# Last down projection: sixteen 128x512 additions and multiplications from VectorE to GpSimd, and a normalisation cut in two

## The chip, the cores and the metric

The program runs on one core of a Trainium2 chip. The metric is the device time of one execution in microseconds, as the median of several runs. Five engines work side by side, each through its own queue in order: TensorE (PE) multiplies matrices, VectorE (DVE) and GpSimd (POOL) work element by element, ScalarE (ACT) applies functions with a scale and a bias, and SyncE (SP) issues transfers. They wait for one another by semaphores.

## The reference, cut to what matters

The reference is a trunk of two layers on 1024 rows of 1024 features. Each layer mixes the rows (a gated delta net, then retention), normalises, runs a feed-forward block with a convolution, and normalises again:

```
gate, up = jnp.split(h @ w_up, 2, axis=-1)
gate = causal_dwconv(gate, conv_w) + conv_b
y = (jax.nn.silu(gate) * up) @ w_down
x = layer_norm(DN_ALPHA * x + (1.0 + g2) * y, ln_g[i, 1], ln_b[i, 1])
```

The change is in the last two lines of the last layer: the product with `w_down` (2816 x 1024), the residual sum, and the layer norm whose result is the output.

## The kernel before, in words

The down projection is `proj_gen`. It makes the product by seven block products in the manner of Strassen (`prods`), on halves of the rows (half 0: rows 0 to 511, half 1: rows 512 to 1023), of the contraction and of the columns (nh 0: columns 0 to 511, nh 1: 512 to 1023). Each product runs over 11 steps j. A step loads a block of activations (`ar`) and makes a block of weights (`Br`, differences of loaded blocks, L1521), and splits each into a high and a low part: ScalarE rounds (L89) to the high part, VectorE subtracts (L90) to get the low part. These pairs are `ab` and `bb`. Four row tiles t of 128 rows then take three matmuls each (L1636), so a step has 12 matmuls. In the last product the first five steps run step by step over all tiles; the last six are kept back and run tile by tile, 18 matmuls to a tile, so that tile 0 is finished first.

What becomes of the products, with the names that matter here:

- The fifth product ends half 0: `f3` and `finish(0, t, 1, ...)` add the residual and make statistics (L1565), then `norm(0, t)` normalises tile t of half 0 and stores it.
- The sixth product (`f7`) gives the right columns of half 1: ScalarE copies the accumulator to `u2` (L1617), VectorE adds it to `p5` (L1618, the tile is called `pa`), and `finish(1, t, 1, p5)` multiplies by the gain row (L1562), adds the residual (L1564) and makes statistics (L1565).
- The seventh product (`f4`) gives the left columns of half 1 in the accumulators `acc`, which lie in PSUM. `finish(1, t, 0, acc)` and `norm(1, t)` follow tile by tile. These are the last steps of the program.

`norm` in the last layer, for one tile: join the statistics (L1570), add epsilon (L1571), GpSimd raises the variance to the power -1/2 (L1572, one element to a partition), VectorE makes a bias (L1578). The left half of the columns (`lo`) is done by VectorE in two passes (L1581, L1582) and stored (L1583). The right half (`hi`) is normalised by ScalarE (L1580), then VectorE multiplies by the gain row (L1584) and adds the bias row (L1585), and it is stored (L1586). The tiles `xt`, `pa`, `rowb`, `ab`, `bb`, `u2` and `mv` lie in SBUF; `acc`, `sc` and `mm` in PSUM.

The order on each engine is not the order of the code. A scheduler sets it when the program is built: it takes instructions out of order where it expects their inputs earlier, and the engines then follow that order whatever really comes first.

Of the kernel before, what the change touches and what calls it, by code (L numbers as in the profile page):

```python
# [12 lines left out]
ALU = mybir.AluOpType  # L13
# [20 lines left out]
def trunk_kernel(ctx: ExitStack, tc, A):  # L34
    nc = tc.nc
    pe, act, dve, pool, sp = nc.tensor, nc.scalar, nc.vector, nc.gpsimd, nc.sync
# [9 lines left out]
    def tl(tag, shape, dt=F32, name=None):  # L46
        return sb.tile(shape, dt, tag=tag, name=name or tag, bufs=BUFS[tag])
# [34 lines left out]
    def hs(half):  # L82
        return slice(half * HALF, (half + 1) * HALF)
# [234 lines left out]
    def normalize(xt, mv, on_act):  # L318
        if on_act:
            dve.scalar_tensor_tensor(mv[:, 2:3], mv[:, 0:1], -1.0, mv[:, 3:4], ALU.mult, ALU.mult)  # L320
            act.activation(xt, xt, AF.Identity, bias=mv[:, 2:3], scale=mv[:, 3:4])
        else:
            dve.tensor_scalar(xt, xt, mv[:, 0:1], mv[:, 3:4], ALU.subtract, ALU.mult)
# [335 lines left out]
    xt = [[tl("lane", [P, 2, HALF], name="xt") for _ in range(4)], [[None, None] for _ in range(4)]]  # L659
# [817 lines left out]
    def proj_gen(nj, ablk, wsrc, slots, xsrc, G, final, ln_next, tag, ltags, dst, key, mm=pe.matmul, gate=None):  # L1477
# [3 lines left out]
        p5 = [pa[2 + t // 2][:, t % 2] for t in range(4)]  # L1481
        u2 = []
# [57 lines left out]
        xts = [[], []]  # L1540
# [16 lines left out]
        def xh(half, t, nh):  # L1557
            x = xts[half][t]
            return x[nh] if isinstance(x, tuple) else x[:, hs(nh)]

        def finish(half, t, nh, c):
            dve.tensor_tensor(c, c, G[nh], ALU.mult)  # L1562
            xv = xh(half, t, nh)
            dve.scalar_tensor_tensor(xv, xv, ALPHA, c, ALU.mult, ALU.add)  # L1564
            dve.bn_stats(stats[half][t][:, nh], xv)  # L1565

        def norm(half, t):
            xt = xts[half][t]
            mv = tl("s8", [P, 4], name="mv")
            dve.bn_aggr(mv[:, 0:2], stats[half][t])  # L1570
            dve.tensor_scalar(mv[:, 2:3], mv[:, 1:2], LN_EPS, None, ALU.add)  # L1571
            pool.tensor_tensor(mv[:, 3:4], mv[:, 2:3], mhalf[:, 0:1], ALU.pow)  # L1572
            if final is None:
                normalize(xt, mv, bal["n"] & 1 << half)
            else:
                (gB, bB), out = final
                r0 = half * HALF + t * P
                dve.scalar_tensor_tensor(mv[:, 2:3], mv[:, 0:1], -1.0, mv[:, 3:4], ALU.mult, ALU.mult)  # L1578
                lo, hi = xh(half, t, 0), xh(half, t, 1)
                act.activation(hi, hi, AF.Identity, bias=mv[:, 2:3], scale=mv[:, 3:4])  # L1580
                dve.scalar_tensor_tensor(lo, lo, mv[:, 0:1], gB[0], ALU.subtract, ALU.mult)  # L1581
                dve.scalar_tensor_tensor(lo, lo, mv[:, 3:4], bB[0], ALU.mult, ALU.add)  # L1582
                sp.dma_start(out[r0:r0 + P, hs(0)], lo)  # L1583
                dve.tensor_mul(hi, hi, gB[1])  # L1584
                dve.tensor_add(hi, hi, bB[1])  # L1585
                sp.dma_start(out[r0:r0 + P, hs(1)], hi)  # L1586

        c11, later = [], []

# [21 lines left out]
        def f3(t, acc):  # L1611
            dve.tensor_add(u2[t], acc, u2[t])
            later.append(lambda: finish(0, t, 1, u2[t]))
            later.append(lambda: norm(0, t))

        def f7(t, acc):
            act.activation(u2[t], acc, AF.Copy)  # L1617
            later.append(lambda: dve.tensor_add(p5[t], u2[t], p5[t]))  # L1618
            if gate:
                later.append(lambda: dve.tensor_add(p5[t], p5[t], p1[t]))  # L1620
            later.append(lambda: finish(1, t, 1, p5[t]))

        def f4(t, acc):
            if gate:
                dve.tensor_add(acc, acc, p1[t])
            finish(1, t, 0, acc)
            norm(1, t)

        outs = []
        prods = [("11", "11", f1, 0, True), ("12", "21", f2, 1, True), ("S1", "T1", f5, 1, True),  # L1630
                 ("S2", "T2", f6, 0, bool(gate)), ("S4", "22", f3, 1, False), ("S3", "T3", f7, 0, False),
                 ("22", "T4", f4, 0, False)]
        banks = [None, None]

# [95 lines left out]
    def layer_tail(i, mix, wout, xsrc, x_mid, x_out, ln_next, final):  # L1730
# [101 lines left out]
        if not final:  # L1832
            wnext_up.append(A["ret_wg"][2])
        gb2 = gain_rows(3, ("mid", i), "hTb") if final else None
        return proj_st(proj_gen(NF // 2, ablk_of(ad, "qkv"), A["ffn_down"][i], slots, xg[i + 1], rows[i, 5],
                       (gb2, x_out) if final else None, ln_next, "hTb", ("hTb", "hTa", 8, 6, "f") if final else ("qkv", "hTa", 8, 4, "0"), x_out, ("out", i)))

# [19 lines left out]
    h0, xts = layer_tail(0, raws, A["gdn_wout"], xin, xs[0], xs[1], next0, False)  # L1857
# [230 lines left out]
    def start_out():  # L2088
        slots = {"c": "hTb", "x": "hTb"}
        mix.append(proj_gen(8, ablk_of(od, "qkv"), A["ret_wout"], slots, xg[0], rows[1, 2], None,  # L2090
                            lambda: mix[1], "hTa", ("qkv", "hTb", 4, 4, "r"), xs[2], ("mid", 1), pm, lambda j: after_ev(("ob", j // 2))))
        assert next(mix[0]) == "ops"
# [131 lines left out]
```

## Time and profile before

| | us |
|---|---|
| median of 3 runs | 2862.41 |
| lowest and highest of them | 2862.29, 2869.69 |
| the profiled execution's own time | 2866.75 |
| its span, first to last instruction | 2865.0 |
| PE busy in the span | 2781.6 (97%) |
| DVE busy | 2186.8 (76%) |
| ACT busy | 1292.3 (45%) |
| POOL busy | 495.2 (17%) |

The profiled execution took 4.34 us more than the median of the runs, and 1.75 us of it lie outside its span. Busy times are averages over the program. Where a tile is named, buffer numbers are left out, so `xt` stands for all the row tiles. A timeline row reads: start, duration, engine, line, operation, output and inputs, shape, and in brackets the idle time before it and what ended it. Rows of one kind that follow each other are merged, with their count behind an x. Instructions on VectorE overlap by about 0.1 us, so the step from one start to the next is the time that one takes in a full queue.

### The profile page before, as it was taken

The page shows a single profiled execution, that of the slowest core. Times are in us where ns is not written, and L with a number is a line of the kernel's source. Part 1 is how long each engine was busy: PE and PEld are TensorE (multiplying, and loading weights), DVE is VectorE, ACT ScalarE, POOL GpSimd, SP SyncE. Part 2 cuts the span into 40 slices and gives each one's busy share as a digit, 9 for nine tenths or more (in the row PEclk, how much of TensorE's full clock was granted, in tenths as well). Part 3 has the DMA queues.
Part 4 walks back from the last instruction along what each step waited for, and adds up shares of the span by engine and source line. Part 5 has one row for each costly group of instructions (what it writes and reads, how often), then busy time and mean ns, then how long its engine had stood idle before and what let it go on. Part 6 is the DMA issues. An engine that isn't in the chain of part 4 may idle for free.

```text
span 2865.0 us, 38941 instructions
## 1 busy us (share of the span) xinstructions
PE 2781.6 (97%) x13594; PEld 2272.3 (79%) x13594; DVE 2186.8 (76%) x3874; ACT 1292.3 (45%) x2377; POOL 495.2 (17%) x517
## 2 busy tenths in 40 slices
PE   8999999999999999999999999999999999999997
PEld 6788888877787878887888887777787788888886
DVE  6797778676788888778677656666788887777869
ACT  3753465344644444545433342222344644445443
POOL 0411311000023222000000002333301033322001
PEclk9999999999999999999999999999999999999999
DMA  8223243273255554945343364665854253435843
GB/s 280 97 97 113 93 133 104 71 247 138 100 181 173 194 181 168 338 134 172 129 147 131 115 199 153 200 208 152 276 192 147 74 195 133 147 136 171 314 147 118
DMA packets 254292, 465.31 MB, mean 162 GB/s; under 512 B 24400, under 2 KB 81104, under 8 KB 254096
## 3 DMA queue, kind: packets, MB, share of 16 engines
q1 hardware_dynamic: 219776, 407.50, 43.2%
q10 hardware_dynamic: 31488, 46.15, 4.4%
q0 software_dynamic: 2832, 9.18, 0.8%
q8 instruction: 107, 1.75, 0.3%
q14 instruction: 89, 0.73, 0.1%
HBM read 346.86 MB, written 115.87 MB: 162 GB/s over the span
## 4 chain that ended last, share of the span: by engine, by line
PE 56%; DVE 22%; DMA 10%; ACT 5%; issue 4%; POOL 1%; SPq 0%; ACTq 0%; DVEq 0%; POOLq 0%
PE acc L747 7%; PE acc L1340 6%; PE acc L110 4%; PE acc L111 4%; PE acc L112 4%; PE acc L1636 4%; PE sc L747 3%; PE sc L1340 3%; DMA mvw<-in_ada_w 2%; DVE qkv L507 2%; DVE o L1787 2%; PE mm L747 2%; DVE wb L90 2%; DMA wr<-in_ffn_up 2%; DVE mm L1394 2%
## 5 line engine op out<-in xcount | busy, mean ns | idle before, releaser
L747 PE MATMUL acc<-hT,wh 128*128 128x512 f32 x960 | 298.4, 392 | 0.0
L1636 PE MATMUL acc<-bb,ab 128*128 128x512 f32 x984 | 231.3, 394 | 4.8 <-DVE ab L90 3.0
L89 ACT ACTIVATE ab<-ar 128x512 fp32r<-128x512 f32 x210 | 131.0, 630 | 222.2 <-PE mm L316 55.1
L1636 PEld LDWEIGHTS acc<-bb,ab 128*128 128x128 f32 x984 | 184.3, 189 | 46.9 <-DVE ab L90 3.1
L747 PEld LDWEIGHTS acc<-hT,wh 128*128 128x128 f32 x960 | 181.4, 189 | 35.1
L90 DVE TENSOR_TENSOR ab<-ar,ab 128x512 fp32r<-128x512 f32 x210 | 149.2, 719 | 70.4 <-ACT ab L89 67.1
L1340 PE MATMUL acc<-T,wb 128*128 128x512 f32 x840 | 202.0, 389 | 0.4 <-DVE wb L90 0.4
L89 ACT ACTIVATE wb<-mm 128x512 fp32r<-128x512 f32 x216 | 124.3, 597 | 169.6 <-DVE mm L1394 158.5
L747 PE MATMUL acc<-hT,wl 128*128 128x512 f32 x480 | 196.6, 410 | 3.6 <-DVE wl L90 2.3
L1340 PEld LDWEIGHTS acc<-T,wb 128*128 128x128 f32 x840 | 157.5, 188 | 33.8 <-ACT o L1788 1.2
L90 DVE TENSOR_TENSOR wl<-wr,wh 128x1024 fp32r<-128x1024 f32 x95 | 119.1, 1254 | 75.6 <-ACT wh L89 75.3
L89 ACT ACTIVATE wh<-wr 128x1024 fp32r<-128x1024 f32 x95 | 100.4, 1057 | 144.7 <-PE acc L747 61.3
L90 DVE TENSOR_TENSOR wb<-wr,wb 128x512 fp32r<-128x512 f32 x162 | 115.9, 716 | 64.7 <-ACT wb L89 64.5
L1818 POOL TENSOR_TENSOR o<-o 128x512 f32<-128x512 f32 x80 | 112.6, 1416 | 268.1 <-ACT pc L1410 173.9
L1787 DVE SCALAR_TENSOR_TENSOR o<-g,vc,o 128x512 f32<-128x512 f32 (+2 forms) x176 | 150.9, 868 | 7.0 <-ACT o L1782 5.8
L90 DVE TENSOR_TENSOR wb<-mm,wb 128x512 fp32r<-128x512 f32 x216 | 145.4, 686 | 7.4 <-ACT wb L89 7.4
L89 ACT ACTIVATE wb<-wr 128x512 fp32r<-128x512 f32 x162 | 101.1, 626 | 93.5 <-PE acc L1340 26.4
L1394 DVE TENSOR_TENSOR mm<-wr 128x512 f32<-128x512 f32 x108 | 86.5, 800 | 70.6 <-DMA wr<-in_ffn_up 56.8
L747 PE MATMUL acc<-wh,hT 128*128 128x512 f32 x384 | 134.8, 413 | 2.0 <-DVE vv L90 2.0
L1410 ACT ACTIVATE pc<-acc 128x512 f32<-128x512 f32 x143 | 84.3, 590 | 107.6 <-PE acc L1340 62.4
L252 DVE SCALAR_TENSOR_TENSOR ada<-mvw,e,ada 128x512 f32<-128x512 f32 x140 | 106.6, 761 | 25.2 <-DMA mvw<-in_ada_w 25.0
L110 PE MATMUL acc<-T,wb 128*128 128x512 f32 x292 | 114.4, 392 | 3.6 <-DVE wb L90 3.5
(677 smaller groups left out, 7361.5 us busy)
## 6 DMA issues: line engine op xcount, KB each, us to landing
wr<-in_ffn_up SPq DMA_DIRECT2D x92, 512.0 KB, 3.9
mvw<-in_ada_w SPq DMA_DIRECT2D x80, 512.0 KB, 4.4
ad<-o SPq DMA_DIRECT2D x154, 256.0 KB, 2.3
ar<-ad SPq DMA_DIRECT2D x154, 256.0 KB, 4.7
Br<-in_ffn_down SPq DMA_DIRECT2D x88, 256.0 KB, 5.1
wr<-in_ret_wv SPq DMA_DIRECT2D x32, 512.0 KB, 3.6
ar<-od SPq DMA_DIRECT2D x56, 256.0 KB, 4.7
wr<-in_gdn_wqkv SPq DMA_DIRECT2D x24, 512.0 KB, 3.8
```

Source lines behind the costliest of these rows:

```text
L89: anchor["sp"] = act.activation(dst_h, src, AF.Copy)
L90: eng.tensor_tensor(dst_l, src, dst_h, ALU.subtract)
L110: mm(acc, wl[:, k], hl[0], start=first, stop=False)
L111: mm(acc, wh[:, k], hl[1], start=False, stop=False)
L112: mm(acc, wh[:, k], hl[0], start=False, stop=last)
L252: dve.scalar_tensor_tensor(a, wr[:, kk], e[:, k:k + 1], a, ALU.mult, ALU.add)
L747: pq(pe.matmul(out, lhsT, rhs, start=start, stop=stop), cost or COST[out.shape[-1]])
L1340: return pe.matmul(*a, skip_group_check=True, **kw)
L1394: dve.tensor_tensor(t, x, y, op)
L1636: return pe.matmul(*args, skip_group_check=True, **kw)
L1787: dve.scalar_tensor_tensor(tv, gv[:, c0 - j:c1 - j], w[:, 2 - j:3 - j], tv, ALU.mult, ALU.add)
L1818: (dve if fp == 0 else pool).tensor_tensor(o[d], o[x], o[y], op)
```

## The change

`norm` is cut into `stat` (statistics and the power) and `apply` (the rest). Where it is the last layer, `f4` puts `apply` of a tile behind `stat` of the next tile in the code. In `apply`, the multiplication and addition on the right half go to GpSimd for the four tiles of half 0 and for tiles 0 and 1 of half 1, and stay on VectorE for tiles 2 and 3 of half 1. The addition of `u2` to `p5` in `f7` also goes to GpSimd in the last layer. That is 12 + 4 instructions of 128x512 elements.

```
-        def norm(half, t):
-            xt = xts[half][t]
+        def stat(half, t):
             mv = tl("s8", [P, 4], name="mv")
             dve.bn_aggr(mv[:, 0:2], stats[half][t])
             dve.tensor_scalar(mv[:, 2:3], mv[:, 1:2], LN_EPS, None, ALU.add)
             pool.tensor_tensor(mv[:, 3:4], mv[:, 2:3], mhalf[:, 0:1], ALU.pow)
+            return mv
+
+        def apply(half, t, mv):
+            xt = xts[half][t]
...
+                eng = dve if half and t > 1 else pool
...
-                dve.tensor_mul(hi, hi, gB[1])
-                dve.tensor_add(hi, hi, bB[1])
+                eng.tensor_tensor(hi, hi, gB[1], ALU.mult)
+                eng.tensor_tensor(hi, hi, bB[1], ALU.add)
                 sp.dma_start(out[r0:r0 + P, hs(1)], hi)
+
+        def norm(half, t):
+            apply(half, t, stat(half, t))
...
-            later.append(lambda: dve.tensor_add(p5[t], u2[t], p5[t]))
+            later.append(lambda: (pool if final else dve).tensor_tensor(p5[t], u2[t], p5[t], ALU.add))
...
             finish(1, t, 0, acc)
-            norm(1, t)
-
+            if not final:
+                norm(1, t)
+                return
+            last.append((t, stat(1, t)))
+            if t:
+                apply(1, *last.pop(0))
+            if t == 3:
+                apply(1, *last.pop(0))
+
+        last = []
```

Line numbers shift: L1571 becomes L1570, the power L1572 becomes L1571, L1578 becomes L1582, L1580 becomes L1584, L1581 and L1582 become L1585 and L1586, L1584 and L1585 become L1588 and L1589, L1618 becomes L1625.

The end of GpSimd's queue before, with the numbers of the buffers (`o` is the feed-forward block's activation, long done by then; mv_24592 to mv_24660 belong to tiles 0 to 3 of half 0, and the four that follow, from mv_25095 on, to half 1):

```order
L1818 TENSOR_TENSOR o_23120<-o_23120,o_23105 128x512
L1818 TENSOR_TENSOR o_23115<-o_23115,o_23105 128x512
L1572 TENSOR_TENSOR mv_24592<-mv_24592,mhalf_80 128x1
L1572 TENSOR_TENSOR mv_24607<-mv_24607,mhalf_80 128x1
L1572 TENSOR_TENSOR mv_24645<-mv_24645,mhalf_80 128x1
L1572 TENSOR_TENSOR mv_24660<-mv_24660,mhalf_80 128x1
L1572 TENSOR_TENSOR mv_25095<-mv_25095,mhalf_80 128x1
```

The same place in GpSimd's queue now, up to the power of the fourth tile of half 0 (xt_23795 and xt_23844 are tiles 0 and 1 of half 0, pa_23281 and pa_23282 hold `p5` of two tiles each):

```order
L1571 TENSOR_TENSOR mv_24592<-mv_24592,mhalf_80 128x1
L1571 TENSOR_TENSOR mv_24607<-mv_24607,mhalf_80 128x1
L1588 TENSOR_TENSOR xt_23795<-xt_23795,rowb_23273 128x512
L1625 TENSOR_TENSOR pa_23281<-u2_24318,pa_23281 128x512
L1625 TENSOR_TENSOR pa_23281<-u2_24326,pa_23281 128x512
L1589 TENSOR_TENSOR xt_23795<-xt_23795,rowb_23276 128x512
L1588 TENSOR_TENSOR xt_23844<-xt_23844,rowb_23273 128x512
L1625 TENSOR_TENSOR pa_23282<-u2_24334,pa_23282 128x512
L1571 TENSOR_TENSOR mv_24645<-mv_24645,mhalf_80 128x1
L1625 TENSOR_TENSOR pa_23282<-u2_24342,pa_23282 128x512
L1589 TENSOR_TENSOR xt_23844<-xt_23844,rowb_23276 128x512
L1571 TENSOR_TENSOR mv_24660<-mv_24660,mhalf_80 128x1
```

The power of tile 2 now stands behind six 128x512 instructions, that of tile 3 behind eight. Behind these rows follow the four of tiles 2 and 3 of half 0, and then, between the powers of half 1, the four of its tiles 0 and 1.

VectorE's queue before, at the last splits of the last product (ab_25068 is the last block of activations that TensorE needs; xt_23896 and xt_23948 are tiles 2 and 3 of half 0, xt_24076, xt_24125, xt_24175 and xt_24226 are right columns of half 1):

```order
L1562 TENSOR_TENSOR pa_23281<-pa_23281,rowb_20841 128x512 x2
L1585 TENSOR_TENSOR xt_23844<-xt_23844,rowb_23276 128x512
L1562 TENSOR_TENSOR pa_23282<-pa_23282,rowb_20841 128x512
L90 TENSOR_TENSOR ab_25039<-ar_25036,ab_25039 128x512
L90 TENSOR_TENSOR ab_25050<-ar_25047,ab_25050 128x512
L1584 TENSOR_TENSOR xt_23896<-xt_23896,rowb_23273 128x512
L1562 TENSOR_TENSOR pa_23282<-pa_23282,rowb_20841 128x512
L90 TENSOR_TENSOR ab_25059<-ar_25056,ab_25059 128x512
L1584 TENSOR_TENSOR xt_23948<-xt_23948,rowb_23273 128x512
L90 TENSOR_TENSOR ab_25068<-ar_25065,ab_25068 128x512
```

The same place now:

```order
L1562 TENSOR_TENSOR pa_23282<-pa_23282,rowb_20841 128x512
L1564 SCALAR_TENSOR_TENSOR xt_24125<-xt_24125,pa_23281 128x512
L90 TENSOR_TENSOR ab_25039<-ar_25036,ab_25039 128x512
L90 TENSOR_TENSOR ab_25050<-ar_25047,ab_25050 128x512
L1582 SCALAR_TENSOR_TENSOR mv_24660<-mv_24660 128x1
L1586 SCALAR_TENSOR_TENSOR xt_23948<-xt_23948,mv_24660,rowb_23276 128x512
L90 TENSOR_TENSOR ab_25059<-ar_25056,ab_25059 128x512
L1564 SCALAR_TENSOR_TENSOR xt_24175<-xt_24175,pa_23282 128x512
L1565 BN_STATS st_24078<-xt_24076 128x6
L1564 SCALAR_TENSOR_TENSOR xt_24226<-xt_24226,pa_23282 128x512
L1565 BN_STATS st_24127<-xt_24125 128x6
L90 TENSOR_TENSOR ab_25068<-ar_25065,ab_25068 128x512
```

All four residual sums L1564 of the right columns of half 1 and two of their statistics L1565 now stand ahead of the last split; before, they stood behind it. Ten moved instructions that stood ahead of the last split are gone from this queue: L1584 of four tiles, L1585 of two, and L1618 of four.

VectorE's queue before, in the normalisation of half 1 (xt_24076 and mv_25095 are tile 0, xt_24125 and mv_25128 tile 1, xt_24174 the left columns of tile 2):

```order
L1562 TENSOR_TENSOR acc_23290<-acc_23290,rowb_20840 128x512
L1570 BN_AGGR mv_25095<-st_24078 128x2
L1570 BN_AGGR mv_25128<-st_24127 128x2
L1564 SCALAR_TENSOR_TENSOR xt_24174<-xt_24174,acc_23290 128x512
L1571 TENSOR_SCALAR mv_25095<-mv_25095 128x1
L1581 SCALAR_TENSOR_TENSOR xt_24076<-xt_24076,mv_25095,rowb_23273 128x512
L1571 TENSOR_SCALAR mv_25128<-mv_25128 128x1
L1581 SCALAR_TENSOR_TENSOR xt_24125<-xt_24125,mv_25128,rowb_23273 128x512
L1565 BN_STATS st_24178<-xt_24174 128x6
L1578 SCALAR_TENSOR_TENSOR mv_25095<-mv_25095 128x1
L1582 SCALAR_TENSOR_TENSOR xt_24076<-xt_24076,mv_25095,rowb_23276 128x512
```

The same place now:

```order
L1562 TENSOR_TENSOR acc_23288<-acc_23288,rowb_20840 128x512
L1564 SCALAR_TENSOR_TENSOR xt_24076<-xt_24076,acc_23288 128x512
L1565 BN_STATS st_24078<-xt_24076 128x6
L1569 BN_AGGR mv_25095<-st_24078 128x2
L1570 TENSOR_SCALAR mv_25095<-mv_25095 128x1
L1585 SCALAR_TENSOR_TENSOR xt_24076<-xt_24076,mv_25095,rowb_23273 128x512
L1582 SCALAR_TENSOR_TENSOR mv_25095<-mv_25095 128x1
L1586 SCALAR_TENSOR_TENSOR xt_24076<-xt_24076,mv_25095,rowb_23276 128x512
L1562 TENSOR_TENSOR acc_23289<-acc_23289,rowb_20840 128x512
L1564 SCALAR_TENSOR_TENSOR xt_24125<-xt_24125,acc_23289 128x512
L1565 BN_STATS st_24127<-xt_24125 128x6
```

Before, work of two tiles was interleaved, so that something stood between a step and the next that needs it. Now tile 0 runs from its sum to its last pass without a break, although the code has `apply` of a tile behind `stat` of the next; tiles 1 and 2 follow in the same way. Only of tile 2 the second pass (L1582, L1586) and the right half (L1588, L1589) stand among tile 3's steps.

## The prediction

> **What bounds the kernel now.** I read the busy time by stretches first, since the whole program says little about its last 50 us.
>
> ```profile
> core 0: us, PE busy (x) PEld busy (x) DVE busy (x) ACT busy (x) POOL busy (x), PEclk, DMA share, GB/s
> 2800.00:2816.50 16.50, 16.50 (x74) 13.66 (x73) 16.50 (x35) 10.27 (x18) 3.20 (x2) 1.00 0.56 171
> 2816.50:2837.00 20.50, 19.76 (x86) 15.74 (x85) 20.50 (x40) 8.67 (x15) 4.66 (x2) 1.00 0.19 72
> 2837.00:2851.00 14.00, 13.74 (x60) 10.69 (x58) 14.00 (x29) 0.27 (x1) 1.72 (x2) 1.00 0.10 37
> ```
>
> VectorE is busy in every instant from 2800 to 2851, and TensorE nearly so. Which waits for which is seen in TensorE's timeline.
>
> ```profile
> 2809.70 26.09 PE L1636 MATMUL acc<-bb,ab 128*128 128x512 f32 x113
> 2836.53 0.97 PE L1636 MATMUL acc<-bb,ab 128*128 128x512 f32 x3 [0.74 <-DVE ab L90]
> 2837.73 13.24 PE L1636 MATMUL acc<-bb,ab 128*128 128x512 f32 x57 [0.23 <-DVE ab L90]
> ```
>
> TensorE runs without a break until 2835.79. Then it waits 0.74 and 0.23 us for the last splits of VectorE, and has 13.24 us of matmuls left; it ends at 2850.97. VectorE's timeline around those splits and at the end:
>
> ```profile
> 2836.36 0.71 DVE L1584 TENSOR_TENSOR xt<-xt,rowb 128x512 f32<-128x512 f32 x1
> 2836.96 0.71 DVE L90 TENSOR_TENSOR ab<-ar,ab 128x512 fp32r<-128x512 f32 x1
> 2837.57 1.92 DVE L1564 SCALAR_TENSOR_TENSOR xt<-xt,pa 128x512 f32<-128x512 f32 x3
> ...
> 2851.99 0.71 DVE L1562 TENSOR_TENSOR acc<-acc,rowb 128x512 f32<-128x512 f32 x1
> ...
> 2857.71 0.22 DVE L1570 BATCH_NORM_AGGREGATE mv<-st 128x2 f32<-128x12 f32 x1
> 2857.97 0.15 DVE L1571 TENSOR_SCALAR mv<-mv 128x1 f32<-128x1 f32 x1
> 2858.04 0.74 DVE L1581 SCALAR_TENSOR_TENSOR xt<-xt,mv,rowb 128x512 f32<-128x512 f32 x1
> 2858.69 0.69 DVE L1584 TENSOR_TENSOR xt<-xt,rowb 128x512 f32<-128x512 f32 x1
> 2859.30 0.16 DVE L1578 SCALAR_TENSOR_TENSOR mv<-mv 128x1 f32<-128x1 f32 x1
> 2859.36 0.75 DVE L1582 SCALAR_TENSOR_TENSOR xt<-xt,mv,rowb 128x512 f32<-128x512 f32 x1
> 2860.03 0.69 DVE L1585 TENSOR_TENSOR xt<-xt,rowb 128x512 f32<-128x512 f32 x1
> 2860.63 0.69 DVE L1584 TENSOR_TENSOR xt<-xt,rowb 128x512 f32<-128x512 f32 x1
> 2861.35 0.69 DVE L1585 TENSOR_TENSOR xt<-xt,rowb 128x512 f32<-128x512 f32 x1
> ```
>
> One 128x512 pass takes 0.60 us from start to start (2836.36, 2836.96, 2837.57). The last split stands at 2836.96, behind other work, so whatever moves it moves TensorE's end. It ends its turn at 2837.57, and VectorE then needs 24.5 us to 2862.04, its last addition's end; that is 11.1 us after TensorE's last matmul. So the end is VectorE's queue twice over: first up to the last split, then from there to the last store. The last two stores:
>
> ```profile
> 2860.74 1.66 SPq L1586 DMA_DIRECT2D out_dram<-xt  x2
> ```
>
> They are issued by 2862.40, and the span ends at 2865.0. I leave this end as it is.
>
> **GpSimd beside VectorE.** The change moves work between two engines, so the first question is whether they run at the same time. GpSimd ran 128x512 additions and multiplications earlier in this program. The group from the page, then pieces of both timelines from another stage:
>
> ```profile
> L1818 POOL TENSOR_TENSOR o<-o 128x512 f32<-128x512 f32 x80 | 112.6, 1416 | 268.1 <-ACT pc L1410 173.9
> ```
>
> ```profile
> 2578.63 1.29 POOL L424 TENSOR_TENSOR xg<-xg,gb 128x512 f32<-128x512 f32 x1 [7.62 <-DMA xg<-xs]
> 2580.01 1.62 POOL L425 TENSOR_TENSOR xg<-xg,gb 128x512 f32<-128x512 f32 x1
> ...
> 2653.25 1.33 POOL L1818 TENSOR_TENSOR o<-o 128x512 f32<-128x512 f32 x1 [0.37 <-DMA ad<-o]
> ```
>
> ```profile
> 2578.46 0.68 DVE L1773 TENSOR_TENSOR g<-acc,pc 128x512 f32<-128x512 f32 x1
> 2579.06 0.69 DVE L1394 TENSOR_TENSOR mm<-mm,wr 128x512 f32<-128x512 f32 x1
> 2579.66 0.82 DVE L90 TENSOR_TENSOR wb<-wr,wb 128x512 fp32r<-128x512 f32 x1
> 2580.40 1.77 DVE L1787 SCALAR_TENSOR_TENSOR o<-g,vc,o 128x512 f32<-128x512 f32 x1
> ...
> 2653.35 1.78 DVE L90 TENSOR_TENSOR bb<-Bw,bb 128x512 fp32r<-128x512 f32 x1
> ```
>
> L424 runs from 2578.63 to 2579.92. The passes at 2578.46 and 2579.06 read one operand from PSUM (`acc`, `mm`) and keep their 0.68 and 0.69 us. L90 at 2579.66 reads two operands from SBUF: it ends at 2580.48, 0.56 after GpSimd's end. L425 in turn ends 1.15 after that L90, L1787 0.54 after L425, and L90 at 2653.35 ends 0.55 after GpSimd (2654.58). So the two exclude each other: a GpSimd pass takes 1.15 us in which a VectorE pass with two SBUF operands stands still, and they take turns.
>
> **The change, up to the last split.** GpSimd could begin when ScalarE has the right half of the first tile:
>
> ```profile
> 2815.38 0.80 ACT L1580 ACTIVATE xt<-xt,mv 128x512 f32<-128x512 f32 x1
> ```
>
> That is 2816.2, and from then on all twelve passes for half 0 and `p5` can come before the last split.
> - Removed ahead of it: L1584 of four tiles, L1585 of two, L1618 of four, 10 x 0.60 = 6.0 us.
> - Set ahead of it by the scheduler: L1564 four times, L1565 twice, 6 x 0.60 = 3.6 us.
> - Holds: nearly all of VectorE's work here (splits, L1562 on `pa`, L1564 on `pa`, L1585, L1586) has two SBUF operands. 12 x 1.15 = 13.8 us. The last two passes meet an L1565, which reads one operand; I take 0.6 off. 13.2 us.
>
> The last split moves by -6.0 + 3.6 + 13.2 = +10.8 us. Bounds: the holds could be 0 (-2.4) or whole (+11.4); I take the value near the upper end, as the rows above show whole holds. Two new waits lie on this stretch. L1562 on `pa` now waits for GpSimd's L1625, with splits queued behind it, and L1582 waits for the power of tiles 2 and 3, which stands behind six and eight passes. While VectorE waits there, GpSimd runs unhindered, so this is not added again. The powers alone look harmful:
>
> ```profile
> 2818.65 4.66 POOL L1572 TENSOR_TENSOR mv<-mv,mhalf 128x1 f32<-128x1 f32 x2 [6.16 <-DVE mv L1571]
> ...
> 2858.26 0.92 POOL L1572 TENSOR_TENSOR mv<-mv,mhalf 128x1 f32<-128x1 f32 x1 [1.36 <-DVE mv L1571]
> ```
>
> One power can take 0.92 us, a pair 4.66 between back-to-back passes of VectorE. If GpSimd's large passes were shut out like that, VectorE would reach L1562 early and stand there while they run: the same turns in another order, worth at most about 1 us either way.
>
> TensorE's remaining 13.24 us begin after the last split, so its end moves from 2850.97 to about 2861.8. ScalarE's split of the same blocks waits for buffers that TensorE frees, and moves along. SyncE's stores wait for GpSimd and not for VectorE; nothing else is queued behind them.
>
> **The change, after the last split.** Of the 24.5 us, 12 passes go: L1584 and L1585 of tiles 0 and 1, two L1585 of half 0, and the six now set ahead. 12 x 0.60 = -7.2 us. In exchange:
> - The order runs tiles 0, 1 and 2 one after another. L1564, L1565 and L1569 wait for the step just before. A step behind its own input takes 0.72 (2860.63 to 2861.35) in place of 0.60, three times a tile: 9 x 0.12 = 1.1. L1570 comes 0.26 after L1569 (2857.71 to 2857.97), where its 0.22 less the usual overlap of 0.1 would be 0.12: 3 x 0.14 = 0.4.
> - L1582 waits for the power with nothing between. From L1581 to L1578 it is 1.26 us above (2858.04 to 2859.30), of which L1584 filled 0.60. That filler is gone for tiles 0, 1 and 3: 3 x 0.6 = 1.8. For tile 2, L1562 of tile 3 fills it.
> - Four GpSimd passes (tiles 0 and 1). They meet L1562 and L1564 on `acc` and L1565 of the next tile, three passes of which none reads two SBUF operands. Two rows above show such PSUM readers unhindered. No row shows L1565 beside a 128x512 pass of GpSimd, so the hold lies between 0 and 4 x 1.15 = 4.6; I take 0.5, for the end of a pass that reaches into L1585.
>
> [...]
>
> Sum of this part: -7.2 + 1.1 + 0.4 + 1.8 + 0.5 = -3.4 us. Its tile chain, some 4.5 us, is longer than TensorE's 18 matmuls (13.24 x 18 / 57 = 4.2), so VectorE and not TensorE sets it.
>
> **Together** +10.8 - 3.4 = +7.4 us: the profiled execution would go from 2866.75 to 2874.2, and the median from 2862.41 to 2869.8. A measurement of this kernel can tell about 0.3% from no change, 8.6 us; the forecast is slower by 0.26% and lies just within that.
>
> **The rivals.**
> 1. *Slower beyond doubt: the tail's holds are whole.* If GpSimd's four passes for tiles 0 and 1 also stop L1565 and the PSUM readers, or fall on L1585 and L1586 instead, the second part gains 4.1 us and the first 0.6: +12.1, 2874.5. It decides from 1.7 us of hold in the tail instead of 0.5. For it: VectorE has no free instant before 2851. Against: the unhindered PSUM readers.
> 2. *They run side by side.* In this stage the passes are on other tiles, and the holds might be small. The splits then come early, TensorE's two waits go (0.97) and it ends at 2850.0. VectorE's last chain behind that, by the order now: L1562, L1564, L1588, L1565, L1589 0.60 each, the last steps of tile 2 0.73, L1569 and L1570 0.33, L1585 to the power 1.26, L1582 and L1586 0.72, 0.25 for ScalarE, then 0.72 and 0.69: 7.7 in place of 11.1. That is -4.3 with the rounding, 2858.1. Against: each of the three VectorE rows with two SBUF operands above stands still for GpSimd.
> 3. *The change does not do what it says.* The tiles are hardly staggered: that is in the order already and in the sum (1.1 + 0.4 + 1.8). If GpSimd is shut out by full queues as the powers were, time moves by less than 1 us from the forecast, 2869 to 2871.
>
> **How the numbers follow.** The forecast has 0.55, of which 0.12 lies above 8.6 us, as the first part's holds (13.2) are uncertain by some 2 us; its own range is 2866 to 2873. Rival 1 has 0.22, rival 2 0.17 (0.02 of it a gain over 8.6), rival 3 0.06 (0.01 above). Slower by over 0.3%: 0.12 + 0.22 + 0.01 = 0.35. Faster by over 0.3%: 0.02. The rest, 0.63, is within. The range for 8 in 10 takes in rival 2's 2858.1 and rival 1's 2874.5: 2857.5 to 2875.
>
> **What would show it.** In the profile of the changed kernel, L90, L1562 on `pa`, L1585 and L1586 between 2816 and 2850 should show 1.7 us instead of 0.7 where a GpSimd pass runs, twelve in all; TensorE should wait some 10 us more for `ab` before its last 57 matmuls; its end should lie about 11 us later, and VectorE's end 7 to 9 us behind it instead of 11. L1565 and the passes on `acc` should keep 0.7. I am wrong if TensorE ends before 2852 (rival 2), or if VectorE's end still lies 11 us or more behind TensorE's (rival 1).

## The result, and the profile after

The changed kernel takes 2873.55 us (median of 20 runs, 2868.54 to 2881.41), the kernel before 2866.7 us (20 runs beside them, 2861.55 to 2872.94). The ratio of the times is 1.0028, with a 95% interval of 1.0022 to 1.0035. So it is slower by 0.28%, some 8 us (the two medians alone differ by 6.85): a little less than the 0.3% that the prediction counted as a difference, but not nothing. The forecast was +7.4 us or +0.26%; it was counted from 2862.41, the median of the first three runs, so the +7.4 and not its 2869.8 is what to compare.

The profiled execution took 2868.67 us, its span is 2866.9. The two profiled executions don't reach the changed place at the same time, for a reason that lies ahead of it: the first power of half 0 starts 5.9 us earlier in the changed kernel. These are its rows, of before and of after, in GpSimd's timeline.

```profile
2807.78 1.00 POOL L1572 TENSOR_TENSOR mv<-mv,mhalf 128x1 f32<-128x1 f32 x1 [153.20 <-DVE mv L1571]
```

```profile
2801.84 1.00 POOL L1571 TENSOR_TENSOR mv<-mv,mhalf 128x1 f32<-128x1 f32 x1 [152.89 <-DVE mv L1570]
...
2814.70 1.74 POOL L1589 TENSOR_TENSOR xt<-xt,rowb 128x512 f32<-128x512 f32 x1
...
2831.55 3.31 POOL L1588 TENSOR_TENSOR xt<-xt,rowb 128x512 f32<-128x512 f32 x1 [5.40 <-ACT xt L1584]
2834.93 2.94 POOL L1589 TENSOR_TENSOR xt<-xt,rowb 128x512 f32<-128x512 f32 x1
...
2847.98 1.29 POOL L1589 TENSOR_TENSOR xt<-xt,rowb 128x512 f32<-128x512 f32 x1
```

Differences of the absolute times would therefore mislead. From here on every place is given as its distance from this power, in every kernel. (Of GpSimd's other rows: a 128x512 pass that VectorE leaves alone takes 1.29 us, in turns with VectorE 1.74; the rows at 2831.55 and 2834.93 waited longer.)

| us after the first power | before | after | difference |
|---|---|---|---|
| what follows the last split on VectorE begins | 29.8 | 38.2 | +8.4 |
| TensorE's last matmul ends | 43.2 | 54.4 | +11.2 |
| VectorE's last addition ends | 54.3 | 62.1 | +7.8 |
| the span ends | 57.2 | 65.05 | +7.85 |

The 7.85 us of the trace lie within what the runs allow (6.3 to 10 us by the interval), so as far as these runs can tell the whole change of time lies in these last 65 us. VectorE's timeline of after shows the first stage, up to the last split (2838.95), and some rows of the tail:

```profile
2810.55 1.25 DVE L1582 SCALAR_TENSOR_TENSOR mv<-mv 128x1 f32<-128x1 f32 x1
2811.73 1.86 DVE L1586 SCALAR_TENSOR_TENSOR xt<-xt,mv,rowb 128x512 f32<-128x512 f32 x1
2813.51 1.78 DVE L90 TENSOR_TENSOR ab<-ar,ab 128x512 fp32r<-128x512 f32 x1
2815.22 1.77 DVE L90 TENSOR_TENSOR bb<-Br,bb 128x512 fp32r<-128x512 f32 x1
...
2822.63 2.39 DVE L90 TENSOR_TENSOR bb<-Br,bb 128x512 fp32r<-128x512 f32 x2
...
2833.62 1.25 DVE L1582 SCALAR_TENSOR_TENSOR mv<-mv 128x1 f32<-128x1 f32 x1
...
2836.66 0.68 DVE L1565 BATCH_NORM_STATS2 st<-xt 128x6 f32<-128x512 f32 x1
2837.27 1.16 DVE L1564 SCALAR_TENSOR_TENSOR xt<-xt,pa 128x512 f32<-128x512 f32 x1
...
2838.95 1.14 DVE L90 TENSOR_TENSOR ab<-ar,ab 128x512 fp32r<-128x512 f32 x1
2840.01 1.27 DVE L1565 BATCH_NORM_STATS2 st<-xt 128x6 f32<-128x512 f32 x2
2841.83 0.70 DVE L1562 TENSOR_TENSOR acc<-acc,rowb 128x512 f32<-128x512 f32 x1 [0.54 <-PE acc L1651]
...
2845.51 0.16 DVE L1582 SCALAR_TENSOR_TENSOR mv<-mv 128x1 f32<-128x1 f32 x1 [0.44 <-POOL mv L1571]
...
2848.10 0.70 DVE L1562 TENSOR_TENSOR acc<-acc,rowb 128x512 f32<-128x512 f32 x1 [1.77 <-PE acc L1651]
...
2855.02 1.07 DVE L1585 SCALAR_TENSOR_TENSOR xt<-xt,mv,rowb 128x512 f32<-128x512 f32 x1
...
2863.25 0.69 DVE L1589 TENSOR_TENSOR xt<-xt,rowb 128x512 f32<-128x512 f32 x1
```

Rows of 1.7 to 1.8 us are a pass of 0.7 that stood still for 1.1; the first is a 128x1 step that takes 0.16 elsewhere (2845.51). There are eight such full holds from 2810.55 to 2825 (one in the pair at 2822.63), one at 2833.62, and two of about 0.5 (2837.27 and 2838.95). L1565 keeps its time beside GpSimd (0.68 at 2836.66, and the pair at 2840.01). Behind the last split VectorE is held only once, for 0.3 us at 2855.02, but it now waits for `acc`, that is for TensorE, which it never did here before. Why it waits is in TensorE's timeline of after:

```profile
2820.45 5.05 PE L1651 MATMUL acc<-bb,ab 128*128 128x512 f32 x21 [1.41 <-DVE ab L90]
2826.99 4.39 PE L1651 MATMUL acc<-bb,ab 128*128 128x512 f32 x18 [1.49 <-DVE ab L90]
2833.14 1.67 PE L1651 MATMUL acc<-bb,ab 128*128 128x512 f32 x6 [1.76 <-DVE ab L90]
2836.19 0.97 PE L1651 MATMUL acc<-bb,ab 128*128 128x512 f32 x3 [1.38 <-DVE ab L90]
2840.14 16.08 PE L1651 MATMUL acc<-bb,ab 128*128 128x512 f32 x57 [2.99 <-DVE ab L90]
```

Five waits for splits, 9.0 us in all where it was 1.0, as VectorE's holds would have it. But the last 57 matmuls, 13.24 us before, take 16.08. The windows of after say why, in the column PEclk (the granted clock as a share of full speed, behind the busy times of the five engines):

```profile
core 0: us, PE busy (x) PEld busy (x) DVE busy (x) ACT busy (x) POOL busy (x), PEclk, DMA share, GB/s
2831.00:2840.00 9.00, 3.02 (x11) 1.53 (x9) 9.00 (x13) 1.80 (x3) 8.29 (x4) 0.97 0.21 83
2840.00:2844.00 4.00, 3.85 (x9) 3.08 (x10) 3.37 (x6) 0.00 (x0) 1.23 (x1) 0.50 0.20 76
2844.00:2848.00 4.00, 4.00 (x14) 3.11 (x14) 1.84 (x5) 0.81 (x1) 2.31 (x3) 0.72 0.17 66
2848.00:2852.00 4.00, 4.00 (x20) 3.30 (x19) 3.32 (x8) 0.02 (x1) 2.26 (x2) 1.00 0.17 66
```

Behind the wait of 2.99 us the clock is 0.50 for all of the first 4 us, in which 9 matmuls begin or run where the last window has 20, and it comes back within the next 4.

### The profile page after: what moved, and what is told of

It reads as the page before. It is cut to its first block, busy times and chain, and to the rows that moved or that the text cites. A ratio compares the mean times of both kernels' runs of the same rounds, so it can differ in the third digit from the quotient of the medians.

```text
span 2866.9 us, 38946 instructions
## 1 busy us (share of the span) xinstructions
PE 2784.4 (97%) x13594; PEld 2276.1 (79%) x13594; DVE 2185.2 (76%) x3858; ACT 1294.6 (45%) x2377; POOL 521.3 (18%) x533
## 4 chain that ended last, share of the span: by engine, by line
PE 63%; DVE 16%; DMA 9%; ACT 5%; issue 4%; POOL 2%; SPq 1%; ACTq 0%; DVEq 0%; POOLq 0%
PE acc L747 10%; PE acc L1340 6%; PE acc L1651 5%; PE acc L110 4%; PE acc L111 4%; PE acc L112 4%; PE sc L747 4%; PE sc L1340 3%; DMA mvw<-in_ada_w 2%; PE mm L747 2%; DVE qkv L507 2%; PE sc L110 2%; PE sc L111 2%; PE sc L112 2%; DVE o L1802 2%
```

## The experiments

The forecast rested on holds that are paid one by one, and it came out almost exactly. It did so with two terms off: the first stage is +8.4 where +10.8 was said, the tail -0.5 where -3.4 was said. The runs below ask whether holds are the cause, what each part brings, and what the tail lost. The first power starts at 2808.89 (d12), 2810.30 (m12), 2804.26 (tail_only), 2816.80 (warm), 2805.54 (p5_only) and 2811.86 (h0_only), and the places are:

| us after the first power | next after the last split | TensorE's end | VectorE's end | span's end |
|---|---|---|---|---|
| before | 29.8 | 43.2 | 54.3 | 57.2 |
| after | 38.2 | 54.4 | 62.1 | 65.05 |
| d12 | 42.8 | 56.6 | 67.5 | 70.4 |
| m12 | 29.8 | 43.2 | 54.25 | 57.2 |
| tail_only | 29.8 | 43.2 | 54.8 | 57.7 |
| p5_only | 34.1 | 48.25 | 57.5 | 60.5 |
| h0_only | 33.5 | 47.8 | 57.0 | 59.9 |
| warm | 38.2 | 51.5 | 59.7 | 62.6 |

**d12: the kernel before, with GpSimd passes and nothing taken from VectorE.** Twelve multiplications of two finished rows into a scratch tile, four behind the power of tile 1 and eight behind that of tile 3 of half 0.

```
+                p = pool.tensor_tensor(mv[:, 3:4], mv[:, 2:3], mhalf[:, 0:1], ALU.pow)
+                if final is not None and not half and t % 2:
+                    with tc.issue_after(p.ins):
+                        for _ in range(4 if t == 1 else 8):
+                            pool.tensor_tensor(tl("t2", [P, HALF], name="dum"), final[0][0][0], final[0][1][0], ALU.mult)
```

> The kernel before, with twelve more 128x512 multiplications on GpSimd into a scratch tile, four behind the power of tile 1 of half 0 and eight behind that of tile 3; nobody waits for them, and VectorE's queue is that of before, instruction by instruction. Theory A, exclusion: each of them that meets a pass with two SBUF operands holds VectorE for about 1.1 us. Ten to twelve holds, the last split 10 to 13 us later, the end 9 to 13 us later (ratio 1.003 to 1.005), VectorE's L90 and L1581 with 1.7 us where one runs. Theory B, VectorE merely waits for slow results of GpSimd: nothing waits for these, so the time is that of before within 0.1%. Theory C, the changed order costs the time: also that of before.

Measured: 2879.67 us, ratio 1.0044 (1.0029 to 1.0060). The end of the first stage moves by 13.0 us, 1.08 for each of the twelve. GpSimd's and VectorE's timelines of d12 (L1576 are the added passes):

```profile
2813.58 6.54 POOL L1576 TENSOR_TENSOR dum<-rowb 128x512 f32<-128x512 f32 x4
...
2828.78 18.80 POOL L1576 TENSOR_TENSOR dum<-rowb 128x512 f32<-128x512 f32 x8
```

```profile
2813.79 1.78 DVE L90 TENSOR_TENSOR bb<-Br,bb 128x512 fp32r<-128x512 f32 x1
2815.49 3.48 DVE L1521 TENSOR_TENSOR Br<-Br,Bw 128x512 f32<-128x512 f32 x2
```

Four passes took 6.54 us and held three VectorE passes in a row and the 128x1 step behind them. The eight took 18.80, more than 8 x 1.7, since two of them waited through several VectorE passes before their turn; each still held VectorE once. So the price comes with GpSimd's passes, and not with a wait for their results, which nobody reads here. One more thing is seen here, in TensorE's timeline and in windows of 3.4 us:

```profile
2821.52 12.79 PE L1640 MATMUL acc<-bb,ab 128*128 128x512 f32 x48 [1.99 <-ACT u L1621]
```

```profile
2818.47:2821.88 3.41, 1.42 (x7) 0.88 (x6) 3.41 (x6) 2.34 (x4) 1.65 (x1) 1.00 0.06 23
2821.88:2825.30 3.42, 3.42 (x10) 2.65 (x9) 3.42 (x9) 3.20 (x7) 1.15 (x1) 0.50 0.34 131
```

Behind a wait of only 1.99 us TensorE's clock stands at 0.50 for 3.4 us. The last section comes back to it.

**m12: the same twelve as fills, which read nothing.**

```
-                            pool.tensor_tensor(tl("t2", [P, HALF], name="dum"), final[0][0][0], final[0][1][0], ALU.mult)
+                            pool.memset(tl("t2", [P, HALF], name="dum"), 0.0)
```

> The same with twelve GpSimd fills (a constant written to 128x512 elements, no SBUF read) in place of the multiplications. [...] If any GpSimd instruction holds VectorE: twelve times 0.5 us, 4 to 6 us later. Theory B and C: the time of before.

Measured: 2865.53 us, ratio 0.9998 (0.9989 to 1.0007), and every place of the table as before. GpSimd's and VectorE's timelines of m12:

```profile
2825.78 3.80 POOL L1576 MEMSET dum<- 128x512 f32 x8
```

```profile
2826.00 1.29 DVE L1622 TENSOR_TENSOR pa<-u,pa 128x512 f32<-128x512 f32 x2
```

Eight fills run in 3.80 us while VectorE's pair with two SBUF operands keeps its 1.29. GpSimd at work beside VectorE cost nothing by itself here: the end of the first stage moved by 0, where the twelve multiplications of d12, which read SBUF, moved it by 13.0. (A fill is also another operation and a shorter one, 0.48 us against 1.29, so the runs alone don't prove that it is the reading.)

**tail_only: only the four passes of tiles 0 and 1 of half 1 go to GpSimd.** The rest is as in the changed kernel, with the eight of half 0 and the sums on `p5` back on VectorE.

```
-                eng = dve if half and t > 1 else pool
+                eng = pool if half and t < 2 else dve
...
-            later.append(lambda: (pool if final else dve).tensor_tensor(p5[t], u2[t], p5[t], ALU.add))
+            later.append(lambda: dve.tensor_tensor(p5[t], u2[t], p5[t], ALU.add))
```

> The change with GpSimd only for tiles 0 and 1 of half 1; half 0 and the sums of p5 stay on VectorE, whose order ahead of the last split is then that of before. Theory A: the last split and TensorE's end as before; after it VectorE has four passes less (-2.4 us) and one or two holds more: -2.5 to +0.5 us, ratio 0.999 to 1.000. Theory C, the cost lies in the order of the tail: as much later as the change, +6 to +8 us.

Measured: 2865.53 us, ratio 1.0001 (0.9989 to 1.0013). Up to the last split nothing moves; VectorE's end moves by +0.5. GpSimd's and VectorE's timelines of tail_only:

```profile
2848.09 2.82 POOL L1588 TENSOR_TENSOR xt<-xt,rowb 128x512 f32<-128x512 f32 x2 [1.17 <-ACT xt L1584]
2850.86 1.71 POOL L1589 TENSOR_TENSOR xt<-xt,rowb 128x512 f32<-128x512 f32 x1
```

```profile
2849.86 1.58 DVE L1585 SCALAR_TENSOR_TENSOR xt<-xt,mv,rowb 128x512 f32<-128x512 f32 x1
...
2853.59 1.21 DVE L1582 SCALAR_TENSOR_TENSOR mv<-mv 128x1 f32<-128x1 f32 x1 [0.44 <-POOL mv L1571]
```

Here two of the four passes fall on L1585 and the 128x1 step L1582, which are held by 0.84 and 1.06. With the wait of 0.44 for the power, and steps that now stand right behind their input, that spends the 4 x 0.60 = 2.4 us that VectorE saves. The same four passes in the changed kernel cost 0.3 (two holds of 0.3 in warm), since there the tiles run one after another and GpSimd works while VectorE reads PSUM (L1562 and L1564 on `acc`, 0.69 to 0.70), does statistics (L1565, 0.69) or waits for `acc`. The tail alone gains nothing.

**p5_only and h0_only: the two parts of the first stage.** p5_only sends only the four sums on `p5` to GpSimd (`eng = dve`, `f7` as changed). h0_only sends only the eight passes of half 0:

```
-                eng = dve if half and t > 1 else pool
+                eng = dve if half else pool
...
-            later.append(lambda: (pool if final else dve).tensor_tensor(p5[t], u2[t], p5[t], ALU.add))
+            later.append(lambda: dve.tensor_tensor(p5[t], u2[t], p5[t], ALU.add))
```

> Of the change, only the four sums of p5 on GpSimd. Theory A: four holds of 1.1 us against four passes of 0.60 saved on VectorE, +2.0 us; by the order the last split also has the four L1564 of the right columns ahead of it, so it comes 4.4 us later and TensorE waits that much more, which is won back behind it: +1.5 to +3.5 us at the end (ratio 1.0005 to 1.0012). Theory B, VectorE waits for GpSimd's results: waits of VectorE at L1562 on pa, with a POOL releaser, make up the loss. If the cost is in the eight passes of half 0 instead: the time of before.

> Of the change, only the eight passes on the right half of half 0 on GpSimd. Theory A: eight passes of 0.60 us saved (-4.8) against five to eight holds of 1.1 us, fewer where GpSimd comes late into a run of two-operand passes and gets in only beside a one-operand pass: 0 to +4 us, ratio 1.000 to 1.0014. No result of these passes is read by VectorE, so under theory B (waits for results) the gain of 4.8 us stays, ratio 0.998 to 0.999.

Measured: p5_only 2871.09 us, ratio 1.0015 (1.0002 to 1.0029); h0_only 2867.1 us, ratio 1.0006 (0.9996 to 1.0016). The runs alone don't tell h0_only from the kernel before, as its interval takes in 1; the places are read from one profiled execution each. From the power on, the spans end 3.2 and 2.7 us later than before. The first stage can be added up for both. In p5_only four sums are gone from VectorE's rows ahead of the last split, four L1564 have come there, and four holds of 1.09 stand in it: -2.4 + 2.4 + 4.4 = +4.4, where +4.3 was measured. In h0_only six passes are gone, three L1564 have come, and there are five holds: -3.6 + 1.8 + 5.5 = +3.7, where +3.7 was measured. GpSimd's timeline and TensorE's of h0_only:

```profile
2838.25 8.97 POOL L1589 TENSOR_TENSOR xt<-xt,rowb 128x512 f32<-128x512 f32 x1
2847.18 1.28 POOL L1588 TENSOR_TENSOR xt<-xt,rowb 128x512 f32<-128x512 f32 x1
```

```profile
2841.31 18.32 PE L1651 MATMUL acc<-bb,ab 128*128 128x512 f32 x66 [3.01 <-DVE ab L90]
```

Only five of eight passes held VectorE in full: L1589 at 2838.25 was kept out for 8.97 us until VectorE came to its statistics, and it and the last two then ran beside passes that kept their time (four L1565 in 2.46 us from 2845.99, then L1562 and L1564 on `acc` with 0.68 and 0.69). And both kernels show what the changed one showed in TensorE: 66 matmuls at the old rate are 13.24 x 66 / 57 = 15.3 us, but here they take 18.3 behind a wait of 3.01. In p5_only it is 18.2 behind 3.69. It costs the two differently: in h0_only VectorE then waits 1.01 + 0.30 us for `acc`, in p5_only not at all.

**warm: the changed kernel with TensorE kept busy.** 22 matmuls on operands already used, into a PSUM tile that nobody reads, stand in TensorE's waits for the last splits.

```
+                warm = mm_tile()
...
+                    if final and p == 6 and t == 0 and j in (7, 9, 10):
+                        for _ in range({7: 6, 9: 5, 10: 11}[j]):
+                            pm_on(warm, prev[0][0][:, 0:P], prev[1][0], start=True, stop=True)
+                    prev = (a, w)
```

> The changed kernel with 22 matmuls more on TensorE, into a free PSUM tile that nobody reads, six, five and eleven of them where TensorE waits for the splits of steps 7, 9 and 10 of the last product (5.0 us at 0.227 us each, less than the 6.1 us of those waits). Theory D, the waits let the granted clock of TensorE fall to 0.50 for some 6 us, which makes the accumulators of tiles 0 and 1 late: with the gaps filled the clock stays at 1.0, the last 57 matmuls take 13.2 instead of 16.1 us, VectorE's waits for TensorE (0.54 and 1.77 us) go, and the end comes about 2.3 us earlier than in the changed kernel (ratio to before 1.002). [...]

Measured: 2873.02 us, ratio 1.0026 (1.0015 to 1.0038). The time alone can't tell this from the changed kernel's 1.0028 (1.0022 to 1.0035): what is at stake is 0.08%. The profile can. TensorE's timeline and windows of warm:

```profile
2851.92 2.69 PE L1651 MATMUL mm<-bb,ab 128*128 128x512 f32 x11
2855.12 13.21 PE L1651 MATMUL acc<-bb,ab 128*128 128x512 f32 x57 [0.52 <-DVE ab L90]
```

```profile
2850.00:2854.00 4.00, 3.77 (x17) 2.74 (x16) 4.00 (x7) 0.65 (x1) 4.00 (x2) 1.00 0.08 30
2854.00:2858.00 4.00, 3.48 (x16) 2.56 (x15) 3.93 (x6) 0.00 (x0) 2.14 (x2) 1.00 0.43 167
```

The clock stays at 1.00 and the 57 matmuls take 13.21 us again. The last split stands where it stood in the changed kernel (38.2), VectorE no longer waits for `acc`, and its end comes 2.4 us sooner. The holds are still there, so they are not what slows the matmuls. The fall of the clock came with TensorE's idle time here, and it cost the tail of the changed kernel's profiled execution 2.4 us.

**turns: when does GpSimd get its turn?** The first stage was mis-sized because some passes waited long and then ran beside passes that kept their time (L1565 at 2836.66 of after, 0.68). A test behind the last output of the kernel before: four stretches of 24 VectorE instructions, beside each five GpSimd passes queued behind one another.

```
+                if kind == "c":
+                    o = dve.tensor_tensor(dd[0], src[0] if not k else dd[0], src[1], ALU.add)
+                elif kind == "s" and k % 4 == 3:
+                    o = dve.tensor_scalar(z[:, 3:4], z[:, 0:1], LN_EPS, None, ALU.add)
+                elif kind == "o" and k % 4 == 3:
+                    o = dve.bn_stats(st[:, 0], src[0])
+                else:
+                    o = dve.tensor_tensor(dd[k % 4], src[0], src[1], ALU.mult)
```

> The kernel before, with a test behind its last output: four stretches of 24 VectorE instructions on scratch tiles, and beside each stretch five GpSimd multiplications of 128x512, queued one behind another and begun within about 1 us of the stretch. In stretch 1 the 24 are passes with two SBUF operands that do not need each other; in stretch 2 each reads what the one before it wrote; in stretch 3 every fourth is a 128x1 step; in stretch 4 every fourth is a statistics pass with one operand. The total time means nothing here (some 80 us are added). Theory A (always turns: a waiting GpSimd pass gets in behind the VectorE pass that is running): in every stretch the five GpSimd passes take about 1.75 us each, 8.7 us in all, and five VectorE passes take 1.75. Theory B (a waiting GpSimd pass gets in only at a gap): in stretch 1 the first GpSimd pass waits until the stretch is over, so it takes more than 10 us; in stretch 2, where a step behind its own input costs 0.72 instead of 0.60, they take turns as in theory A; in stretch 3 and 4 one GpSimd pass gets in at each 128x1 step or one-operand pass, every 1.9 to 2.4 us. If stretch 2 is shut out as well, only the 128x1 step and the one-operand pass are gaps.

Measured, in GpSimd's and VectorE's timelines of turns (L2143 are the five passes, `zo` the 128x1 step ahead of the fourth stretch's):

```profile
2861.75 8.48 POOL L2143 TENSOR_TENSOR qq<-src,src 128x512 f32<-128x512 f32 x5
...
2882.90 7.93 POOL L2143 TENSOR_TENSOR qq<-src,src 128x512 f32<-128x512 f32 x5
...
2905.18 8.38 POOL L2143 TENSOR_TENSOR qq<-src,src 128x512 f32<-128x512 f32 x5
...
2921.12 1.78 POOL L2140 TENSOR_TENSOR zo<-zo 128x1 f32<-128x1 f32 x1 [6.96 <-DVE zo L2134]
2922.86 7.93 POOL L2143 TENSOR_TENSOR qq<-src,src 128x512 f32<-128x512 f32 x5
```

```profile
2862.36 19.86 DVE L2153 TENSOR_TENSOR dd<-src,src 128x512 f32<-128x512 f32 x24
```

The whole took 2942.55 us in its one execution. Theory B falls. In all four stretches the five passes take 7.9 to 8.5 us, 1.6 to 1.7 each, also where 24 passes stand ready without a gap: 24 x 0.60 = 14.4, and the 5.4 us above it are five holds of 1.08. Queued behind one another, GpSimd's passes took turns with VectorE's in every stretch. But the step `zo`, which found VectorE in a run of three passes, was let in only at the statistics pass behind them (1.78 where its like in the other stretches takes 0.51 to 0.63). So being passed over does happen, here too; what decides when is not settled by these runs.

## Why the prediction came out, point by point

- **Exclusion and its price.** Right in kind, and the size nearly: 1.15 us was read from other stages, 1.08 to 1.09 is what d12, turns and the changed kernel show. In m12 GpSimd's fills, which read nothing, held nothing (VectorE's pair beside them kept its 1.29 us); whether it is the reading itself these runs leave open.
- **The first stage, +10.8.** The terms -6.0 and +3.6 stand. The holds, 13.2, were mis-sized: eight full ones make 8.65, the one at 2833.62 makes 1.09, the two partial ones 0.94, together 10.7. Then -6.0 + 3.6 + 10.7 = +8.3, and +8.4 was measured. Of the 2.5 us too many about 0.7 are the price of a hold (1.15 for 1.09), and about 1.8 are holds that did not come: of twelve passes nine held VectorE in full where all but a half were counted. The prediction saw that GpSimd might be shut out and put it at 1 us at most, "the same turns in another order". It left out where a pass lands that has been shut out. In the changed kernel two landed beside L1565, which kept its 0.68 us (2836.66, 2838.34), and the passes behind it were held for 0.48 and 0.46 instead of 1.09. The 0.6 that the prediction took off for L1565 was its author's estimate; the rows of before that it shows have no L1565 beside a 128x512 pass of GpSimd.
- **Queue effects.** The two new waits ahead of the last split, for GpSimd's sums L1625 and for the powers of tiles 2 and 3, were left out of the sum, rightly: no row of VectorE there waits for GpSimd.
- **The tail, -3.4.** As VectorE's own queue this was right: with TensorE's clock kept up (warm) the tail takes 59.7 - 38.2 = 21.5 us instead of 24.5, which is -3.0. Its small terms hold as well: the waits for the power are 3 x 0.44 = 1.3 (1.8 was said), the hold on L1585 0.3 (0.5, which was an estimate too: L1565 kept 0.69 beside GpSimd in this tail). What failed is the step "TensorE's remaining 13.24 us begin after the last split" and with it "VectorE and not TensorE sets it". The 13.24 were taken from a kernel in which TensorE had not waited longer than 0.74 us. With the wait of 2.99 us the clock fell, they became 16.08, and VectorE waited 0.54 + 1.77 + 0.17 = 2.5 us for `acc`. Measured: -0.5.
- **The sum.** +7.4 was said, +7.85 was measured. That the two are so close is luck: an error of -2.4 in the first stage met one of +2.9 in the tail. The mechanism of the first stage, holds of VectorE for each GpSimd pass, is not luck; the clock was not foreseen at all. The marker "TensorE's end about 11 us later" came true (+11.2) for a wrong reason: +8.4 by the splits and +2.8 by the clock. The marker "waits some 10 us more for `ab`" was the one that told: it is 8.1. "VectorE's end 7 to 9 us behind it" was 7.7.
- **The rivals.** Holds throughout the tail (rival 1) are excluded by L1565's 0.68 and the single hold of 0.3; tail_only shows that they come, 1.9 us of them, where the passes fall on L1585 and L1582 instead. Side by side (rival 2) is excluded by d12. Of rival 3, GpSimd was shut out in places (the rows at 2831.55 and 2834.93), and the holds that did not come, about 1.8 us, are more than the 1 us that was said for it. No run takes the cut into `stat` and `apply` alone; in tail_only, which has it, the last split and TensorE's end stand as before.
- **The parts.** p5_only +3.2, h0_only +2.7 and tail_only +0.5 make 6.4 of the 7.85. Their first stages nearly add up (4.3 + 3.7 = 8.0 of 8.4), their tails don't: -1.1, -1.0 and +0.5 make -1.6, where the changed kernel has -0.5. Each has its own order on VectorE, and the waits for `acc` differ (2.5 us in the changed kernel, 1.3 in h0_only, none in the other two); no run separates these. None of the parts shows a gain, and no version here beats the kernel before.

## What to carry over

Moving a two-operand pass from VectorE to GpSimd freed 0.60 us of VectorE here and took 1.08 to 1.09 back with each full hold of a VectorE pass that reads two SBUF operands. Beside PSUM readers (0.69 to 0.70 us in the changed kernel's tail), statistics (0.68 to 0.69) and idle time it took nothing back, but no run here shows that it pays. A stage that is made to wait may also change the price of what follows (57 matmuls took 16.08 us instead of 13.24 behind the wait of 2.99), so a duration is carried over from a profile only if the waits ahead of it stay as they were. When a forecast's total is right, its terms are still worth checking: here two errors of 2.4 and 2.9 us nearly cancelled.

## What the hardware did unexpectedly

- TensorE's granted clock fell to 0.50 with single waits of 2.99 us (the changed kernel), 3.01 (h0_only) and 3.69 (p5_only) and stayed there until some 6 us after the matmuls went on, which cost 2.8 to 3.0 us of matmuls each time. The length of a single wait did not decide: the clock fell with 1.99 us in d12, and stayed at 1.00 through waits of 1.4 to 1.8 us in the changed kernel and one of 2.58 us in warm. Worked out from the means of 1 us windows, fall and return lie 3.4 and 10.2 us apart in d12 and 6.8 to 6.9 in the changed kernel, p5_only and h0_only. These are two stretches of the changed kernel, each as long as the shortest of those times, the last of them just ahead of the fall at 2839.44:

```profile
2832.62:2836.03 3.41, 1.67 (x6) 1.05 (x6) 3.41 (x5) 0.81 (x1) 3.33 (x2) 1.00 0.07 25
2836.03:2839.44 3.41, 0.97 (x3) 0.48 (x3) 3.41 (x6) 0.00 (x0) 3.41 (x2) 1.00 0.21 79
```

In the first TensorE was busy for 1.67 of 3.41 us, and the clock stayed; in the second for 0.97, and it fell. In d12 it fell behind a stretch with 1.42 of 3.41 us (2818.47 to 2821.88), and in warm it stayed at 1.00 through one with 1.42 of 4.00 (2838 to 2842). What decides whether the clock falls is not shown by these runs.
- The fall cost the tail only where VectorE came to wait for TensorE. The changed kernel's tail lost 2.4 us to it, with 2.5 us of waits for `acc`. In d12 TensorE waited 9.23 us and its clock fell too, but VectorE's tail, there as long as before, grew by only 0.2 us; in p5_only VectorE did not wait for `acc` at all.
- A GpSimd pass that takes 1.29 us alone stood for 8.97 us in h0_only (2838.25) while VectorE ran two-operand passes, though in the four stretches of the run turns the two engines alternated, at 1.6 to 1.7 us a pass.
